# A ninth Strassen pair in gate and up, and three down products whose left operands are made in the down stage

## The chip, the cores and the metric

The kernel runs on one core of a Trainium2 chip. The metric is the device time of one execution in microseconds. A core has a matrix engine (TensorE, PE in the rows, with PEld for its weight loads), a vector engine (VectorE, DVE), an activation engine (ScalarE, ACT), GpSimd (POOL) and a queue engine (SyncE, SP); the DMAs that SP, ACT and POOL issue share sixteen DMA engines. Each engine works through its own instructions in order and waits on semaphores for the others.

## The reference

A trunk of two layers on x of 512 tokens by 1024 channels, in float32. Layer 0 mixes tokens by causal pooling, layer 1 by differential attention; after each mixer comes a SwiGLU feed-forward of width 2816, each with a scaled residual and a LayerNorm.

```python
for i in range(DEPTH):
    h = _multiscale_pool(...) if i % 2 == 0 else _diff_attention(...)
    x = _layernorm(ALPHA * x + h, ln_mix_g[i], ln_mix_b[i])
    x = _layernorm(ALPHA * x + _swiglu(x, w_gate[i], w_up[i], w_down[i]), ln_ffn_g[i], ln_ffn_b[i])

def _swiglu(x, w_gate, w_up, w_down):
    return (jax.nn.silu(x @ w_gate) * (x @ w_up)) @ w_down
```

The change lies in the two feed-forward layers alone.

## The kernel before

**Three matmuls for one.** Every float32 operand is held as two parts, a high one (a cast by ScalarE) and a low one (the rest, made by VectorE as the value less the high part). A product is high by high, high by low and low by high (`mm3`, line 180). So each 128x1024 chunk of weights that arrives costs one ScalarE cast and one VectorE subtraction (`split`, line 148) before PE can use it. There is another way (line 164, for thirteen chunks of the attention stage): ScalarE casts the chunk and writes its negative into the low part, and a DMA from GpSimd adds the chunk from memory once more, so VectorE has no work with it.

**Gate and up.** The 2816 hidden channels are 22 blocks of 128. Block k and block k + 11 form pair k, eleven pairs in all. A pair is worked in one of two ways. A *plain* pair is two pieces f (f0 and f1 are pair 0, f2 and f3 pair 1, f4 and f5 pair 2), each with one gate and one up product of 24 matmuls over 512 tokens (`plain`, line 986; `gated` multiplies them). A *Strassen* pair p takes seven products in place of eight half-size ones, each of 24 matmuls over 256 tokens (`strassen`, line 1006; `half_product`, line 908). Its weights are sums of the four chunks that arrive (VectorE, line 697), and its right operands sums of quarters of x (`sums_of_x`). Three pairs are plain, eight are Strassen's. The first two of the eight (`PRE`) have two of their seven products at the start of the stage and five later. `ORDER` sets the order of the pieces; `steps` holds the sums, casts and low parts ahead of PE by the lookahead of `ahead`.

**What the down stage needs from before.** The down product is Strassen's too: seven products P1, Q5, P6, Q3, P7, P2, Q4 (`DOWN`), each of six *items* (`PAIRS`: five with two blocks, one with one), 42 items in all, numbered d_0 to d_41 (P6 is d_12 to d_17, Q3 d_18 to d_23, P7 d_24 to d_29). An item has a *weight* (sums of down weights, or a block of them) and a *left* operand (sums of quarters of the hidden values), each in two parts. The weight sums are made during gate and up (`weight_sums`, `sum_terms`, line 814): GpSimd loads the terms of set k, adds one by DMA, VectorE adds twice (lines 816 and 817), ScalarE's queue stores to `tsum`. The lefts of Q3 and P7 are made there too: after each pair, `sum_hidden` (line 836) makes two sums on VectorE (lines 842 to 845), ScalarE casts them, VectorE makes the low halves (line 849) and ScalarE's queue stores both parts to `ssum`.

**The down stage.** `multiply` (line 1075) runs an item's matmuls: 12 of 512 columns for two blocks. Ahead of it `prepare(j + 5, j + 4)` (line 890) makes the weight of item j + 4 (`split_item`, line 858: cast on ScalarE, low part on VectorE) and the left of item j + 3 (`left`, line 871). There are six weight pairs, so a weight's tiles come free when PE has ended the item six before. Lefts of Q3 and P7 are loaded from `ssum` by GpSimd (line 878). The left of P6 is subtracted in place by VectorE (line 886), then cast and split; the other lefts are cast and split as they are. Between products VectorE adds results into the residual (line 1073) and takes statistics (line 222). The affine step of the preceding LayerNorm on the residual (lines 260 and 261) is done in half gate and up, half the down stage (`AFFINE`).

## Time and profile before

| what | value |
|---|---|
| three timed runs, us | 934.22, 936.23, 933.59 |
| their median, us | 934.22 |
| the profiled execution: span from first to last instruction, us | 933.1 |
| mean granted TensorE clock | 0.998 |
| HBM read, written | 179.96 MB, 36.72 MB |
| layer 0 gate and up | about 34 to 265 us |
| layer 0 down | 265 to about 364 us |
| attention | about 364 to 593 us |
| layer 1 gate and up, down, end | about 593 to 821, to about 910, to 933 us |

For the profiled execution the profile gives the span alone. A row of the timeline gives start, duration, engine, source line, operation, what is written and read, and in brackets how long the engine stood idle before it and what ended that. A row of the windows gives busy time of each engine in a stretch with the count of instructions, the granted clock, the DMA engines' busy share and GB/s. A row of the chain gives start, duration, engine, what is written, line and count. Matmul durations in a timeline row overlap, so the pace of PE is taken from chain rows.

### The profile page before, as it was taken

The page shows a single profiled execution, that of the slowest core. Times are in us where ns is not written, and L with a number is a line of the kernel's source. Part 1 is how long each engine was busy: PE and PEld are TensorE (multiplying, and loading weights), DVE is VectorE, ACT ScalarE, POOL GpSimd, SP SyncE. Part 2 cuts the span into 40 slices and gives each one's busy share as a digit, 9 for nine tenths or more (in the row PEclk, how much of TensorE's full clock was granted, in tenths as well). Part 3 has the DMA queues.
Part 4 walks back from the last instruction along what each step waited for, and adds up shares of the span by engine and source line. Part 5 has one row for each costly group of instructions (what it writes and reads, how often), then busy time and mean ns, then how long its engine had stood idle before and what let it go on. Part 6 is the DMA issues. An engine that isn't in the chain of part 4 may idle for free.

```text
span 933.1 us, 14897 instructions
## 1 busy us (share of the span) xinstructions
PE 921.9 (99%) x5662; PEld 824.1 (88%) x5662; DVE 798.9 (86%) x1185; ACT 521.0 (56%) x827; POOL 127.8 (14%) x153
## 2 busy tenths in 40 slices
PE   8999999999999999999999999999999999999996
PEld 8998989999988888888888888988999999988885
DVE  6989798999878887968989886889798999977888
ACT  6663444455554456776878863843445554654361
POOL 4131211110101201200211100201112110001101
PEclk9999999999999999999999999999999999999999
DMA  8388999986869989876576522487899996869963
GB/s 236 116 278 263 297 290 299 293 265 230 259 197 312 357 279 250 221 190 171 143 157 157 152 88 84 136 290 217 265 300 303 268 302 204 257 205 329 360 209 101
DMA packets 87909, 217.65 MB, mean 233 GB/s; under 512 B 15348, under 2 KB 26868, under 8 KB 87838
## 3 DMA queue, kind: packets, MB, share of 16 engines
q1 hardware_dynamic: 45148, 123.46, 39.2%
q0 software_dynamic: 18912, 58.47, 25.5%
q10 hardware_dynamic: 23778, 34.78, 10.5%
q8 instruction: 44, 0.72, 0.3%
q14 instruction: 27, 0.22, 0.1%
HBM read 179.96 MB, written 36.72 MB: 232 GB/s over the span
## 4 chain that ended last, share of the span: by engine, by line
PE 86%; DVE 8%; ACT 3%; issue 1%; DMA 1%; ACTq 0%; POOL 0%; DVEq 0%; POOLq 0%
PE A L919 18%; PE P L1086 14%; PE C L919 9%; PE Q L1086 6%; PE B L919 5%; PE va L1242 2%; PE s L1311 2%; PE q L181 2%; PE q L183 2%; PE k L181 2%; PE k L183 2%; PE q L182 2%; PE k L182 2%; PE u L181 1%; PE u L183 1%
## 5 line engine op out<-in xcount | busy, mean ns | idle before, releaser
L697 DVE TENSOR_TENSOR raw<-raw,raw 128x1024 f32<-128x1024 f32 x64 | 78.0, 1221 | 6.8 <-DMA raw<-in_wall 5.9
L155 ACT CAST xs<-hid 128x512 fp32r<-128x512 f32 (+1 forms) x60 | 34.7, 581 | 24.4 <-DVE hid L886 24.4
L156 DVE TENSOR_TENSOR xs<-hid,xs 128x512 fp32r<-128x512 f32 (+1 forms) x60 | 38.3, 641 | 7.8 <-ACT xs L155 7.8
L1331 ACT ACTIVATE p<-p,mn 128x128 f32<-128x128 f32 (+3 forms) x64 | 35.3, 552 | 14.1 <-DVE mn L1326 14.1
L847 ACT CAST v<-u 128x512 fp32r<-128x512 f32 x22 | 13.7, 621 | 43.4 <-DVE u L845 43.4
L878 POOL DMA_DIRECT2D xs<-ssum x24 | 17.5, 727 | 140.3 <-PE Q L1086 67.9
L810 POOL DMA_DIRECT2D b<-in_wall x20 | 15.1, 813 | 142.2 <-DVE g_23l L703 33.2
L810 POOL DMA_DIRECT2D hid<-in_wall x24 | 19.0, 834 | 98.7 <-DMA tsum<-hid 27.4
L1326 DVE CUSTOM_DVE_ANT_0 p<-s,bias 128x128 f32<-128x128 f32 (+3 forms) x64 | 28.0, 485 | 1.1 <-PE s L1311 1.1
L231 POOL TENSOR_TENSOR rs<-rs,mhalf 128x1 f32<-128x1 f32 x16 | 12.6, 787 | 103.6 <-DVE rs L230 96.2
L282 ACT ACTIVATE y<-pt,bT,gT 128x128 f32<-128x128 f32 x40 | 15.1, 456 | 15.9 <-PE pt L268 15.8
L222 DVE BATCH_NORM_STATS2 st<-res 128x6 f32<-128x512 f32 x32 | 22.2, 694 | 1.1
L1028 ACT COPY hid<-C 128x512 f32<-128x512 f32 x16 | 9.4, 588 | 23.6 <-PE C L919 14.1
L762 ACT CAST xs<-hid 128x1024 fp32r<-128x1024 f32 x8 | 8.4, 1051 | 22.0 <-DVE hid L780 10.6
L811 POOL DMA_DIRECT2D b<-in_wall x10 | 12.3, 1228 | 60.8 <-DMA b<-in_wall 60.8
L1042 ACT ACTIVATE sg<-A 128x512 f32<-128x512 f32 x16 | 9.5, 596 | 19.5 <-PE A L919 19.5
L811 POOL DMA_DIRECT2D hid<-in_wall x12 | 14.8, 1236 | 35.5 <-DMA hid<-in_wall 35.5
L1345 DVE SCALAR_TENSOR_TENSOR p<-p,sm,p 128x128 f32<-128x128 f32 (+3 forms) x32 | 17.6, 551 | 1.1
L156 POOL TENSOR_TENSOR sql<-sq,sqh 128x512 fp32r<-128x512 f32 x7 | 9.3, 1329 | 60.5 <-ACT sqh L155 60.5
L1035 DVE TENSOR_TENSOR hid<-C,hid 128x512 f32<-128x512 f32 x16 | 11.0, 688 | 7.4 <-PE C L919 4.9
L261 DVE TENSOR_TENSOR res<-res,gb 128x512 f32<-128x512 f32 (+1 forms) x20 | 16.0, 799 | 0.7
L849 DVE TENSOR_TENSOR v<-u,v 128x512 fp32r<-128x512 f32 x22 | 15.1, 685 | 1.4 <-ACT v L847 1.4
(1212 smaller groups left out, 3583.6 us busy)
## 6 DMA issues: line engine op xcount, KB each, us to landing
raw<-in_wall SPq DMA_DIRECT2D x130, 512.0 KB, 5.5
r<-tsum SPq DMA_DIRECT2D x40, 512.0 KB, 4.3
hid<-in_wall POOLq DMA_DIRECT2D x36, 512.0 KB, 6.0
b<-in_wall POOLq DMA_DIRECT2D x30, 512.0 KB, 6.8
r<-in_wall SPq DMA_DIRECT2D x30, 512.0 KB, 6.1
tsum<-hid ACTq DMA_DIRECT2D x24, 512.0 KB, 6.2
ssum<-v ACTq DMA_DIRECT2D x22, 512.0 KB, 4.7
tsum<-b ACTq DMA_DIRECT2D x20, 512.0 KB, 4.7
```

What stands on the lines that cost most here:

```text
L155: nc.scalar.copy(dst_h, src)
L156: (low or nc.vector).tensor_tensor(dst_l, src, dst_h.bitcast(F32), op=ALU.subtract)
L181: nc.tensor.matmul(acc, ah, bh, start=start, stop=False)
L182: nc.tensor.matmul(acc, ah, bl, start=False, stop=False)
L183: nc.tensor.matmul(acc, al, bh, start=False, stop=stop)
L697: tt(t, raws[pair[0]], raws[pair[1]], op=ALU.add)
L810: nc.gpsimd.dma_start(out=t[:, j], in_=src[:, j])
L811: nc.gpsimd.dma_start(out=t[:, 0], in_=src[:, :, 1], accum_op=ALU.add)
L919: nc.tensor.matmul(acc[:, f * 256 : (f + 1) * 256], w[:, c], x[:, kk, :], start=start and i == 0, stop=stop and i == len(todo) - 1, skip_g ...
L1086: nc.tensor.matmul(accs[s], x[:, k, r], y[:, c], start=first and k == 0 and e == 0, stop=last and k == m - 1 and e == 2, skip_group_check= ...
L1326: nc.vector.tensor_tensor_reduce(out=p, in0=accs[c], in1=biases[h][:, w - 1 :: -1] if w < S else biases[h][:, ::-1], op0=ALU.add, op1=ALU. ...
L1331: nc.scalar.activation(p, p, AF.Exp, bias=mn[:, q, c : c + 1], scale=-1.0, accum_out=sm[:, q, c : c + 1],)
```

## The change

Pair 1 (f2 and f3) stays plain, pair 2 becomes a Strassen pair, and the order of the first pieces is new. `sum_hidden` keeps one subtraction in place, which P6 and the others need, and no longer makes, casts or stores anything; `ssum` is gone. In the down stage `left` makes Q3's left as the sum of a quarter of the hidden values and P6's left, and P7's as the negative of P6's left less another quarter; both are then cast and split like the rest. For items 0, 2 and 4 of P6, Q3 and P7 (`BY_DMA`) the weight's low part is made by ScalarE and an accumulating DMA. All eight halves of the affine step come after f3 and p4 to p10. Weight sums begin one piece later and follow every piece from f1 to p9; the odd sets use a tile of their own instead of rows of `hid` or the tile of the LayerNorm's scales.

```diff
-SPLIT = (3, 4, 5, 6, 7, 8, 9, 10)
+SPLIT = (2, 3, 4, 5, 6, 7, 8, 9, 10)
-SUMS = 1
-NO_SUMS = (3, 3, 10)
-SPARED = {2: 6}
+SUMS = {1: (2, 1), 2: (2, 1)}
+NO_SUMS = ("f0", "p10")
+BY_DMA = {"P6": (0, 2, 4), "Q3": (0, 2, 4), "P7": (0, 2, 4)}
-ORDER = "f0 f1 f2 f3 p3 f4 p4 f5 p5 p6 p7 p8 p9 p10".split()
+ORDER = "f0 f1 f2 p2 f3 p3 p4 p5 p6 p7 p8 p9 p10".split()
-AFFINE = {("P6", 2): (0, 1), ("P6", 3): (1, 1), ("Q3", 1): (2, 0), ("Q3", 2): (3, 0)}
+AFFINE = {u: (i // 2, i % 2) for i, u in enumerate("f3 p4 p5 p6 p7 p8 p9 p10".split())}
...
             def sum_hidden(k):
-                first, second = hid[:, k, :256], hid[:, k, 256:]
-                a12, a22 = hid[:, k + HALF, :256], hid[:, k + HALF, 256:]
...
-                tt(u[:, 0, :], first, second, op=ALU.subtract)
-                tt(second, second, a22, op=ALU.subtract)
-                tt(u[:, 1, :], a12, first, op=ALU.subtract)
-                tt(u[:, 1, :], u[:, 1, :], second, op=ALU.add)
-                yield
-                nc.scalar.copy(v[:, :, 0, :], u)
-                yield
-                tt(v[:, :, 1, :], u, v[:, :, 0, :].bitcast(F32), op=ALU.subtract)
-                yield
-                nc.scalar.dma_start(out=ssum[:, :, :, k, :], in_=v.bitcast(F32))
+                tt(hid[:, k, 256:], hid[:, k, 256:], hid[:, k + HALF, 256:], op=ALU.subtract)
...
             def split_item(j):
...
-                if final and j == len(items) - 1:
+                if i in BY_DMA.get(p, ()) or final and j == len(items) - 1:
                     nc.scalar.copy(h, drops[j])
                     nc.scalar.mul(l, drops.pop(j), -1.0)
-                    nc.gpsimd.dma_start(
-                        out=l, in_=tsum[2, len(PAIRS) - 1, :, :w].bitcast(F32R), accum_op=ALU.add
-                    )
+                    nc.gpsimd.dma_start(out=l, in_=source(j).bitcast(F32R), accum_op=ALU.add)
                 else:
                     split(h, l, drops.pop(j))
...
-                if p in ("P7", "Q3"):
-                    nc.gpsimd.dma_start(out=t.bitcast(F32), in_=ssum[:, 0 if p == "P7" else 1, :, r, :])
...
+                if p == "P6":
+                    tt(src, hid[:, r, 256:], src, op=ALU.subtract)
+                elif p == "Q3":
+                    src = fp.tile([P, 2, 256], F32, tag="u", name=f"u{layer}_{j}")[:, :m]
+                    tt(src, hid[:, q, :256], hid[:, r, :256], op=ALU.add)
+                elif p == "P7":
+                    nc.vector.scalar_tensor_tensor(
+                        src, src, -1.0, hid[:, q, 256:], op0=ALU.mult, op1=ALU.subtract
+                    )
+                split(t[:, 0], t[:, 1], src)
...
             for kind, i in units(layer):
                 (plain if kind == "f" else strassen)(i)
+                unit = f"{kind}{i}"
+                if unit not in NO_SUMS:
+                    weight_sums()
+                if unit in AFFINE:
+                    affine(n - 1, *AFFINE[unit])
```

How the instructions stand is shown at three places. In the rows, d_12h and d_12l are the high and low part of item 12's weight, r_12 is the chunk that arrived for it, xs holds the lefts and hid the hidden values.

On ScalarE in layer 0's down stage, from item 12 (the first of P6), before:

```order
L155 CAST d_12h<-r_12_3086 128x1024
L155 CAST xs_538<-hid_537 128x256
L155 CAST d_13h<-r_13_3106 128x1024
L155 CAST xs_538<-hid_537 128x512
L155 CAST d_14h<-r_14_3124 128x1024
L155 CAST xs_538<-hid_537 128x512
L155 CAST d_15h<-r_15_3144 128x1024
```

and in the changed kernel:

```order
L846 CAST d_12h<-r_12_3097 128x1024
L847 ACTIVATE d_12l<-r_12_3097 128x1024
L155 CAST xs_538<-hid_537 128x256
L155 CAST d_13h<-r_13_3117 128x1024
L155 CAST xs_538<-hid_537 128x512
L846 CAST d_14h<-r_14_3135 128x1024
L847 ACTIVATE d_14l<-r_14_3135 128x1024
L155 CAST xs_538<-hid_537 128x512
```

Every second weight has a second ScalarE pass over its chunk, which stands ahead of the next left's cast.

On VectorE at the passage from P6 to Q3 in the same stage (L886 and L1073 are P6's left and the residual addition), before:

```order
L156 TENSOR_TENSOR d_17l<-r_17_3187,d_17h 128x512
L886 TENSOR_TENSOR hid_537<-hid_537 128x2x256
L156 TENSOR_TENSOR xs_538<-hid_537,xs_538 128x512
L156 TENSOR_TENSOR d_18l<-r_18_3208,d_18h 128x1024
L886 TENSOR_TENSOR hid_537<-hid_537 128x256
L156 TENSOR_TENSOR xs_538<-hid_537,xs_538 128x256
L260 TENSOR_TENSOR res<-res,gb_3164 128x512
L261 TENSOR_TENSOR res<-res,gb_3164 128x512
L156 TENSOR_TENSOR d_19l<-r_19_3229,d_19h 128x1024
```

and in the changed kernel (L865 is P6's left, L868 Q3's):

```order
L156 TENSOR_TENSOR d_17l<-r_17_3196,d_17h 128x512
L865 TENSOR_TENSOR hid_537<-hid_537 128x2x256
L156 TENSOR_TENSOR xs_538<-hid_537,xs_538 128x512
L865 TENSOR_TENSOR hid_537<-hid_537 128x256
L156 TENSOR_TENSOR xs_538<-hid_537,xs_538 128x256
L156 TENSOR_TENSOR d_19l<-r_19_3239,d_19h 128x1024
L868 TENSOR_TENSOR u_18_3327<-hid_537 128x512
L156 TENSOR_TENSOR xs_538<-u_18_3327,xs_538 128x512
L868 TENSOR_TENSOR u_19_3350<-hid_537 128x512
L156 TENSOR_TENSOR xs_538<-u_19_3350,xs_538 128x512
L156 TENSOR_TENSOR d_21l<-r_21_3278,d_21h 128x1024
```

The low parts of items 18 and 20 and the affine rows are gone from VectorE, and each left of Q3 has its sum and its low part there.

On VectorE at the end of pair 5 in layer 0's gate and up (the gate's products L1055 and L1056, the down weights' sums L816 and L817, weights' low parts g), before:

```order
L1055 TENSOR_TENSOR hid_537<-sg_5_0_1771,hid_537 128x2x256
L1056 TENSOR_TENSOR hid_537<-sg_5_1_1797,hid_537 128x2x256
L816 TENSOR_TENSOR hid_537<-hid_537 128x512
L817 TENSOR_TENSOR hid_537<-hid_537 128x512
L703 TENSOR_TENSOR g_38l<-raw_1642,g_38h 128x1024
L842 TENSOR_TENSOR u_5_1846<-hid_537 128x256
L843 TENSOR_TENSOR hid_537<-hid_537 128x256
L844 TENSOR_TENSOR u_5_1846<-hid_537 128x256
L845 TENSOR_TENSOR u_5_1846<-u_5_1846,hid_537 128x256
L703 TENSOR_TENSOR g_39l<-raw_1478,g_39h 128x1024
L703 TENSOR_TENSOR g_40l<-raw_1674,g_40h 128x1024
L849 TENSOR_TENSOR v_5_1847<-u_5_1846,v_5_1847 128x2x256
```

and in the changed kernel (the same sources stand at L1028, L1029, L814 and L815):

```order
L1028 TENSOR_TENSOR hid_537<-sg_5_0_1827,hid_537 128x2x256
L1029 TENSOR_TENSOR hid_537<-sg_5_1_1853,hid_537 128x2x256
L835 TENSOR_TENSOR hid_537<-hid_537 128x256
L814 TENSOR_TENSOR hid_537<-hid_537 128x512
L815 TENSOR_TENSOR hid_537<-hid_537 128x512
L260 TENSOR_TENSOR res<-res,gb_530 128x512
L261 TENSOR_TENSOR res<-res,gb_530 128x512
L703 TENSOR_TENSOR g_41l<-raw_1699,g_41h 128x1024
```

Four operations of the hidden sums and one low half have left the pair's end; one subtraction and a half of the affine step have come.

81 lines of the change are left out of this document (26 added, 55 removed).

## The prediction

> **What bounds the kernel now.** I read the page's head first, then the chain of waits, then the busy time by stage.
>
> ```profile
> span 933.1 us, 14897 instructions
> PE 921.9 (99%) x5662; PEld 824.1 (88%) x5662; DVE 798.9 (86%) x1185; ACT 521.0 (56%) x827; POOL 127.8 (14%) x153
> 605.53 5.47 PE g L725 x24
> 649.08 2.87 PE A L919 x24
> 309.98 14.96 PE Q L1086 x66
> 324.94 38.08 PE P L1086 x168
> 92.00:144.00 52.00, 51.13 (x338) 46.97 (x337) 44.73 (x55) 21.65 (x27) 7.91 (x9) 1.00 0.91 282
> 182.00:222.00 40.00, 40.00 (x334) 39.88 (x334) 38.79 (x49) 20.68 (x27) 2.96 (x4) 1.00 0.82 252
> 295.00:310.00 15.00, 15.00 (x68) 12.43 (x67) 12.18 (x18) 8.09 (x11) 4.35 (x6) 1.00 0.92 326
> 310.00:325.00 15.00, 15.00 (x67) 12.39 (x67) 12.89 (x16) 5.21 (x6) 3.62 (x5) 1.00 0.96 364
> ```
>
> TensorE is the bound. It idles 11.2 us of 933.1, and the chain shows its pace: 24 matmuls of 512 columns take 5.47 us where they start (38.08 / 168 = 0.227 us each in the long run), 24 of 256 columns take 2.88 us (0.120 each). So there are two ways to move the time: fewer or cheaper matmuls, or operands that come late. The window rows (columns: window, PE, PEld, DVE, ACT and POOL busy with counts, clock, DMA share, GB/s) say how near the second is. VectorE is busy 38.8 of 40 us in the middle of gate and up; PE loses 0.9 us in the window from 92 to 144, and nothing in the down stage, where DMA is 92 to 96% busy.
>
> **What the change takes off PE.** By the orders, each layer loses 96 matmuls of 512 columns (one pair's plain products) and gains 168 of 256 columns (seven half products). 96 x 0.227 = 21.8 us, 7 x 2.88 = 20.2 us: 1.6 us a layer, **3.2 us** in all. Nothing lies beside it, since PE is the bound.
>
> **Gate and up: what VectorE gives and gets.**
>
> ```profile
> 59.13 0.40 PE L181 MATMUL g<-xt,g_6h 128*128 128x512 f32 x1
> 60.36 0.69 DVE L260 TENSOR_TENSOR res<-res,gb 128x512 f32<-128x512 f32 x1
> 67.56 1.23 DVE L703 TENSOR_TENSOR g_9l<-raw,g_9h 128x1024 fp32r<-128x1024 f32 x1 [0.93 <-ACT g_9h L700]
> 116.75 1.23 DVE L703 TENSOR_TENSOR g_19l<-raw,g_19h 128x1024 fp32r<-128x1024 f32 x1 [1.17 <-ACT g_19h L700]
> 120.23 0.42 DVE L842 TENSOR_TENSOR u<-hid 128x256 f32<-128x256 f32 x1
> 121.82 1.22 DVE L703 TENSOR_TENSOR g_22l<-raw,g_22h 128x1024 fp32r<-128x1024 f32 x1
> 123.70 0.69 DVE L816 TENSOR_TENSOR b<-b 128x512 f32<-128x512 f32 x1
> 109.34 1.23 DVE L697 TENSOR_TENSOR raw<-raw,raw 128x1024 f32<-128x1024 f32 x1 [2.37 <-DMA raw<-in_wall]
> 111.96 1.23 DVE L697 TENSOR_TENSOR raw<-raw,raw 128x1024 f32<-128x1024 f32 x1 [1.40 <-DMA raw<-in_wall]
> ```
>
> Four operations of a pair's hidden sums take 1.6 us (120.23 to 121.82) and the low half of v about 0.6, eleven times a layer; one of 0.4 stays. That frees 11 x 1.8 = 20 us of VectorE. The new pair adds four weight sums, three low halves and two half-row operations, 7 x 1.14 + 2 x 0.6 = 9 us (a 1.22 us operation lets the next start after 1.14, as 0.69 lets it after 0.60), and the moved affine steps 4 x 1.3 = 5 us. VectorE ends some 6 us a layer lighter, hidden under PE either way.
>
> The new order asks for the weight sums sooner: p2 comes after f2. From layer 0's first gate (60.4 us) to the low half that p4's third product needs, the new VectorE order holds 37 operations of 1.14, nine of 0.60, three of 0.35 and ten of 0.66: 55 us. PE needs that half 66 us on (f1 starts at 59.1; two plain pieces and p2 end at 95.3, f3 106.2, p3 120.6, two products more 126.4). In the like stretch of before, 60.4 to g_19l's end, VectorE stood in seven waits, from g_9l's 0.93 to g_19l's 1.17, about 8 us together; the two for DMA above are 3.8 of them. 55 + 8 leaves 3 us. Bounds: 0.9 us is gained if no loss stays, 3 us are lost if the 8 become 14 (rival 3). I take 0.
>
> **The down stage: where I expect the loss.** Operands of item j are made while PE is five items back, because six weight pairs rotate. One item of two blocks is 12 matmuls, 2.72 us. For P6 the trace shows the ring that makes them:
>
> ```profile
> 282.81 1.05 ACT L155 CAST d_12h<-r 128x1024 fp32r<-128x1024 f32 x1 [0.60 <-PE Q L1086]
> 285.53 1.05 ACT L155 CAST d_13h<-r 128x1024 fp32r<-128x1024 f32 x1 [1.36 <-PE Q L1086]
> 289.17 0.62 ACT L155 CAST xs<-hid 128x512 fp32r<-128x512 f32 x1 [2.59 <-DVE hid L886]
> 289.69 1.04 ACT L155 CAST d_14h<-r 128x1024 fp32r<-128x1024 f32 x1
> 290.77 1.23 DVE L156 TENSOR_TENSOR d_14l<-r,d_14h 128x1024 fp32r<-128x1024 f32 x1 [0.26 <-ACT d_14h L155]
> 291.91 0.68 DVE L886 TENSOR_TENSOR hid<-hid 128x512 f32<-128x512 f32 x1
> 300.41 0.62 ACT L155 CAST xs<-hid 128x512 fp32r<-128x512 f32 x1 [2.74 <-DVE hid L886]
> 300.94 0.62 ACT L155 CAST d_17h<-r 128x512 fp32r<-128x512 f32 x1
> 303.52 1.04 ACT L155 CAST d_18h<-r 128x1024 fp32r<-128x1024 f32 x1
> 294.85 0.39 PE L1086 MATMUL P<-d_12h,xs 128*128 128x512 f32 x1
> 309.81 0.39 PE L1086 MATMUL Q<-d_18h,xs 128*128 128x512 f32 x1
> 335.88 0.39 PE L1086 MATMUL P<-d_28l,xs 128*128 128x512 f32 x1
> ```
>
> Cast of a left operand to cast of the next weight 0.52, to its low half 1.08, to the next left sum 1.14, to that one's cast about 0.72: 3.46 us an item against PE's 2.72. So P6 already eats its lead: weight 13 is cast 12.0 us ahead of its use (285.53 against 297.57, one item after 294.85), weight 18 only 6.3. Q3 and P7 now win it back, as their lefts come by DMA. The change makes Q3 and P7 like P6 and takes three low halves of each product off VectorE; ScalarE writes the negated weight instead, and an accumulating DMA finishes it. What that costs, the attention stage shows (its own by-DMA weights):
>
> ```profile
> 413.40 1.05 ACT L165 CAST w81h<-raw 128x1024 fp32r<-128x1024 f32 x1
> 414.35 1.06 ACT L166 ACTIVATE w81l<-raw 128x1024 fp32r<-128x1024 f32 x1
> 415.70 0.87 POOL L167 DMA_DIRECT2D w81l<-in_wall  x1 [19.51 <-ACT w81l L166]
> DMA to landing us min/median/max: 6.1/7.5/9.7
> DMA to landing us min/median/max: 5.8/7.4/12.8
> DMA to landing us min/median/max: 4.6/6.4/7.7
> ```
>
> The three landing rows are, in turn, these thirteen accumulates of 512 KB (line 167), the 22 accumulates of gate and up (line 811), and the plain loads of lefts that GpSimd issued in layer 0's down stage (line 878).
>
> Ring for two items, one by DMA and one not: cast to weight cast 0.52, to the negation 0.95, to the next left's cast 0.95, to the other weight's cast 0.52, to its low half 1.08, to the left sum 1.14, to its cast 0.72 = 5.9 us, against PE's 5.44. A pair with the half item takes 5.0 (0.62 for 1.05 and 0.60 for 1.14) and the one after it 5.7, with 0.7 more where the two residual additions stand between. That is 5.9 + 5.0 + 5.7 + 0.7 = 17.3 us a product; PE takes 14.96. From the cast of d_12 at 282.8 (the same as before, where ScalarE waits for PE) I get 300.7 for d_18 (the first product 17.8, with the start's waits), 318.0 for d_24 and 329.6 for d_28. The negation ends 2.0 us after: 331.6. PE wants its low half at 335.88. **4.3 us are there; needed are 0.3 to the issue (415.41 to 415.70) and the landing.** The nearest row in kind and load is line 811's, 7.4: short by 3.4 us. Shortfalls of items before it are part of the same 3.4, because PE's delay gives lead back. The ends: 4.6 (a plain load) leaves 0.6, 5.8 gives 1.8, 9.7 gives 5.7. Two layers, the same code, the like DMA share: **6.8 us** (1.2 to 11.4).
>
> [...]
>
> What else moves costs nothing, with its cover: twelve loads of lefts a layer go and nine accumulates come, so GpSimd's queue holds fewer issues; eleven stores of v go from ScalarE's queue; the affine rows that leave the down stage give VectorE 5 us there, outside the ring; the final scale's load moves ahead, where its tile is free. Without PE's cover of gate and up, the 9 us of the new pair's vector work would be the price.
>
> **Sum.** 933.1 - 3.2 + 0 + 6.8 = 936.7 for the profiled span. The runs' median, 934.22, is 1.1 above that span, so 937.8.
>
> **The rivals.**
> [...]
> 2. *Even.* Landing of 5.5 to 6.9 us: 1.5 to 3 us lost a layer, 931.0 + 3.0 to 931.0 + 6.0 = 934 to 937. For it: the plain loads' 6.4 in this very stage. Against it: both accumulate rows have medians of 7.4 and more.
> 3. *The early order starves.* In layer 0 VectorE stands at p3's weight sums until the accumulate of that set has landed. Store 6.2, load 6.0 and accumulate 7.4 follow one another there, some 21 us with issues, between two sets that the new order puts 15 us of PE time apart (p2 to p3). It decides from 6 us of such waiting; PE loses what exceeds the 3 us left, 3 us. On top of the forecast: 941. Before, sets 3 and 5 stood 23 us apart on VectorE (123.70 and 146.91), with no wait.
>
> ```profile
> 146.91 0.68 DVE L816 TENSOR_TENSOR b<-b 128x512 f32<-128x512 f32 x1
> tsum<-hid ACTq DMA_DIRECT2D x24, 512.0 KB, 6.2
> hid<-in_wall POOLq DMA_DIRECT2D x36, 512.0 KB, 6.0
> ```
>
> **Numbers.** About 0.3%, 2.8 us, can be told from no change. The forecast (landing above 7 us) has 0.45, rival 3 0.07, rival 2 0.25, rival 1 0.23. Hence slower 0.52, within 0.25, faster 0.23. The likeliest case alone spans 937 to 942.5; with both signs the range goes from rival 1's 931 to the 9.7 us landing, 931 + 11.4 = 942.4.
>
> **What would show it.** PE matmuls of P7 (and the end of Q3) that wait for a low half written by DMA, first at d_18 to d_24, up to 3.4 us a layer; the first five products of the down stage taking 78 us a layer instead of 74.8; GpSimd's issues of d_28l at about 332; gate and up 1.6 us shorter a layer, the window from 92 to 144 still with under 1 us of idle PE. [...]

## The result and the profile after

The changed kernel takes 946.33 us (median of 4 runs, 944.15 to 948.28) against 933.9 us of the kernel before beside it (932.43 to 936.23): a ratio of 1.014, 95% interval 1.0121 to 1.0159. It is slower, and 4 us above the upper end of the predicted range. The profiled execution took 948.28 us, the longest of the four, and the stages below, which are read from it, sum to 13.4 us, 1 us more than the medians differ by. Here is the head of the page after:

```profile
span 946.5 us, 15095 instructions
...
PE 923.6 (98%) x5806; PEld 830.3 (88%) x5806; DVE 788.2 (83%) x1145; ACT 546.4 (58%) x859; POOL 125.5 (13%) x147
```

From its chain of waits, the rows where PE's pace changes (start, duration, the bank of PE's result memory that is written, matmuls):

```profile
131.51 5.49 PE C L905 x24
137.00 3.14 PE A L905 x24
140.14 2.88 PE B L905 x24
```

And the windows that were shown of before, with the same columns:

```profile
92.00:144.00 52.00, 48.22 (x336) 45.95 (x335) 42.66 (x47) 21.74 (x26) 10.80 (x12) 0.93 0.94 298
182.00:222.00 40.00, 40.00 (x336) 40.00 (x335) 36.19 (x40) 19.04 (x25) 2.72 (x3) 1.00 0.71 212
295.00:310.00 15.00, 15.00 (x67) 12.41 (x67) 10.16 (x16) 9.88 (x13) 1.68 (x2) 1.00 0.99 249
310.00:325.00 15.00, 13.17 (x57) 10.24 (x55) 10.27 (x15) 9.13 (x14) 2.51 (x3) 1.00 1.02 261
325.00:340.00 15.00, 13.29 (x56) 10.47 (x57) 10.71 (x16) 9.09 (x12) 1.68 (x2) 1.00 0.94 243
```

PE's idle time has doubled, from 11.2 to 22.9 us (946.5 - 923.6). In layer 0 it lies in two places: 3.8 us in the window from 92 to 144, where the mean clock is 0.93 as well (24 half matmuls that elsewhere take 2.88 us took 5.49 and 3.14), and 1.8 and 1.7 us in the windows of Q3 and P7. PE's waits over both layers, in total, times and longest (us), name them:

```profile
PE C L905 <- ACT hid L1003: 5.1, 2, 2.8
PE Q L1061 <- DMA d_20l<-in_wall: 2.9, 2, 1.6
PE P L1061 <- DMA d_26l<-tsum: 2.6, 2, 1.7
...
PE A L905 <- DVE hid L1012: 0.9, 1, 0.9
PE Q L1061 <- DMA d_22l<-in_wall: 0.6, 1, 0.6
PE P L1061 <- DMA d_24l<-tsum: 0.4, 1, 0.4
```

The next table counts from one fixed matmul of PE to another: layer 0's gate and up from the transposes behind its first half product (9 us into the stage), layer 1's from f0's first full-width product, the down stage from its first matmul; the five down products are P1 to P7.

| stage, us | before | changed | difference | predicted |
|---|---|---|---|---|
| gate and up, layer 0 | 221.9 | 225.6 | +3.7 | -1.6 |
| five down products, layer 0 | 74.8 | 79.4 | +4.6 | +3.4 |
| gate and up, layer 1 | 215.3 | 217.4 | +2.1 | -1.6 |
| five down products, layer 1 | 74.8 | 78.6 | +3.8 | +3.4 |
| all else | 346.3 | 345.5 | -0.8 | 0 |

The down stage went as forecast and somewhat further. Gate and up, taken at no loss, lost 5.3 and 3.7 us against its forecast. What stands there at p4, the third Strassen pair, in layer 0 (VectorE, then ScalarE, then PE in the timeline; start, duration, and idle time before with its releaser):

```profile
124.42 1.23 DVE L703 TENSOR_TENSOR g_24l<-raw,g_24h 128x1024 fp32r<-128x1024 f32 x1
125.56 0.68 DVE L1028 TENSOR_TENSOR hid<-hid 128x512 f32<-128x512 f32 x1
...
127.23 0.68 DVE L814 TENSOR_TENSOR hid<-hid 128x512 f32<-128x512 f32 x1
...
128.56 1.22 DVE L697 TENSOR_TENSOR raw<-raw,raw 128x1024 f32<-128x1024 f32 x1
129.86 1.04 ACT L700 CAST g_28h<-raw 128x1024 fp32r<-128x1024 f32 x1 [4.01 <-DVE raw L697]
130.87 0.58 ACT L1003 COPY hid<-C 128x512 f32<-128x512 f32 x1
131.51 0.79 PE L905 MATMUL C<-xs,g_25h 128*128 128x256 f32 x2 [2.84 <-ACT hid L1003]
```

p4's fourth product goes into the bank of its second, which ScalarE must copy out first (L1003). On ScalarE's queue that copy stands behind the cast of g_28h, p4's seventh operand, which waits 4.01 us for VectorE's sum. VectorE makes that sum behind p3's last results (from 125.56) and a row of weight sums (the two adds of one set, L814 and L815), without a gap.

### The profile page after: what moved, and what is told of

Same layout as the page of the kernel before. It is cut to its first block, busy times and chain, and to the rows that moved or that the text cites. A ratio compares the mean times of both kernels' runs of the same rounds, so it can differ in the third digit from the quotient of the medians.

```text
span 946.5 us, 15095 instructions
## 1 busy us (share of the span) xinstructions
PE 923.6 (98%) x5806; PEld 830.3 (88%) x5806; DVE 788.2 (83%) x1145; ACT 546.4 (58%) x859; POOL 125.5 (13%) x147
## 4 chain that ended last, share of the span: by engine, by line
PE 76%; DVE 11%; DMA 5%; issue 4%; ACT 4%; ACTq 0%; DVEq 0%; POOL 0%; POOLq 0%
PE A L905 19%; PE C L905 10%; PE P L1061 9%; PE B L905 5%; PE Q L1061 2%; DMA d_26l<-tsum 2%; PE s L1282 2%; DVE raw L697 1%; PE q L181 1%; PE q L183 1%; PE k L181 1%; PE k L183 1%; PE q L182 1%; PE k L182 1%; PE u L181 1%
## 5 line engine op out<-in xcount | busy, mean ns | idle before, releaser
L697 DVE TENSOR_TENSOR raw<-raw,raw 128x1024 f32<-128x1024 f32 x72 | 87.8, 1221 | 5.9 <-DMA raw<-in_wall 4.8
L156 DVE TENSOR_TENSOR xs<-hid,xs 128x512 fp32r<-128x512 f32 x72 | 46.1, 642 | 21.6 <-ACT xs L155 21.6
L155 ACT CAST xs<-hid 128x512 fp32r<-128x512 f32 x72 | 41.6, 580 | 30.0 <-DVE hid L870 17.9
L808 POOL DMA_DIRECT2D b<-in_wall x24 | 18.0, 793 | 154.6 <-DMA tsum<-b 78.1
L808 POOL DMA_DIRECT2D hid<-in_wall x20 | 15.0, 751 | 104.7 <-DVE hid L814 40.8
L1003 ACT COPY hid<-C 128x512 f32<-128x512 f32 x18 | 10.6, 587 | 29.4 <-PE C L905 21.1
L1005 ACT COPY hid<-A 128x512 f32<-128x512 f32 x18 | 10.6, 587 | 27.0 <-PE A L905 27.0
L1017 ACT ACTIVATE sg<-A 128x512 f32<-128x512 f32 x18 | 10.7, 596 | 23.7 <-PE A L905 23.7
L809 POOL DMA_DIRECT2D b<-in_wall x12 | 14.7, 1227 | 62.5 <-DMA b<-in_wall 62.5
L1012 DVE TENSOR_TENSOR hid<-hid,A 128x512 f32<-128x512 f32 x18 | 12.3, 681 | 7.0 <-PE A L905 6.9
L156 POOL TENSOR_TENSOR sql<-sq,sqh 128x512 fp32r<-128x512 f32 x7 | 9.3, 1326 | 60.2 <-ACT sqh L155 60.2
L261 DVE TENSOR_TENSOR res<-res,gb 128x512 f32<-128x512 f32 (+1 forms) x20 | 16.0, 799 | 0.7
L260 DVE TENSOR_TENSOR res<-res,gb 128x512 f32<-128x512 f32 (+1 forms) x20 | 15.8, 791 | 0.0
L156 DVE TENSOR_TENSOR xs<-u,xs 128x512 fp32r<-128x512 f32 (+1 forms) x12 | 7.8, 648 | 9.6 <-ACT xs L155 9.6
```

Source lines behind the costliest of these rows:

```text
L155: nc.scalar.copy(dst_h, src)
L156: (low or nc.vector).tensor_tensor(dst_l, src, dst_h.bitcast(F32), op=ALU.subtract)
L697: tt(t, raws[pair[0]], raws[pair[1]], op=ALU.add)
L808: nc.gpsimd.dma_start(out=t[:, j], in_=src[:, j])
```

## Experiments on the down stage

The table gives every run: the median, the ratio to the kernel before beside it with its 95% interval, and the stages as above. In a kernel with added lines the profile's line numbers stand up to 15 higher than in the changed kernel.

| run | us | ratio, interval | gate and up 0 | down 0 | gate and up 1 | down 1 |
|---|---|---|---|---|---|---|
| changed kernel | 946.3 | 1.0140 (1.0121-1.0159) | 225.6 | 79.4 | 217.4 | 78.6 |
| e10_leftfirst | 958.1 | 1.0269 (1.0247-1.0291) | 223.3 | 88.8 | 217.4 | 83.1 |
| e4_nodma | 960.3 | 1.0294 (1.0274-1.0315) | 223.3 | 86.0 | 217.5 | 86.2 |
| e13_sumearly | 938.0 | 1.0056 (1.0042-1.0071) | 224.7 | 74.8 | 217.4 | 76.3 |
| e14_two | 938.1 | 1.0058 (1.0041-1.0075) | 224.5 | 74.8 | 216.4 | 75.6 |
| e5_eight | 941.4 | 1.0090 (1.0072-1.0108) | 220.4 | 78.8 | 216.3 | 78.6 |
| e1_queue | 946.0 | 1.0137 (1.0114-1.0160) | 224.8 | 79.2 | 216.9 | 78.5 |
| e21_steps | 946.1 | 1.0133 (1.0113-1.0153) | 223.6 | 79.0 | 217.7 | 79.4 |
| e7_affine | 944.4 | 1.0122 (1.0106-1.0139) | 223.6 | 81.1 | 216.1 | 78.8 |
| e18_relief | 950.5 | 1.0193 (1.0172-1.0214) | 223.5 | 79.1 | 220.3 | 79.5 |
| e23_three | 935.1 | 1.0026 (1.0012-1.0039) | 224.0 | 74.8 | 217.9 | 75.3 |
| e24_three_two | 935.5 | 1.0023 (1.0012-1.0035) | 222.3 | 74.8 | 216.3 | 74.8 |
| e31_noadds | 930.8 | 0.9959 (0.9945-0.9974) | 220.3 | 74.8 | 215.1 | 74.8 |
| e32_noaccum | 935.5 | 1.0016 (1.0002-1.0030) | 223.2 | 74.8 | 217.9 | 74.8 |
| e33_f2late | 935.7 | 1.0017 (1.0002-1.0031) | 223.1 | 74.8 | 216.8 | 74.8 |
| e36_order_all | 937.4 | 1.0045 (1.0030-1.0061) | 224.9 | 74.8 | 217.0 | 74.9 |
| e35_order | 948.8 | 1.0165 (1.0148-1.0182) | 224.7 | 79.1 | 220.0 | 78.4 |
| e38_pooladds | 955.9 | 1.0235 (1.0210-1.0259) | 233.8 | 74.8 | 224.5 | 75.9 |
| e39_pooladds2 | 949.6 | 1.0173 (1.0143-1.0203) | 226.8 | 74.8 | 222.3 | 75.5 |

The changed kernel, e10, e4, e13 and e14 have the same code in gate and up. Their layer 0 values, 223.3 to 225.6, show how far single executions differ there, so a difference of up to 2 us between two rows of that column proves nothing; medians decide. Much of the spread is PE's clock: behind the wait at p4 two products took 5.49 and 3.14 us in the changed kernel at a clock of 0.50, and 3.14 and 2.88 in e10, where it stayed at 1.00 (see the last section).

**The left operand ahead of the weights.** In `prepare`:

```diff
+                while prepared[1] < min(lefts, prepared[0]):
+                    left(prepared[1])
+                    prepared[1] += 1
                 while prepared[0] < min(upto, len(items)):
```

> Only the order inside the function that prepares the down stage's items is changed: the left operand of item j+3 is made ahead of the weights of item j+4, not behind them. In the changed kernel ScalarE's cast of a left operand waits 1.89 us at every second item for VectorE's sum (L865, L868, L870), which stands behind the low half (1.22 us) of the item before, which waits for ScalarE's cast of it: a ring of 5.7 to 5.9 us for two items, against 5.44 us that PE takes for them; so the accumulate of d_20l is issued at 310.39 and lands some 7.7 us later, when PE has been waiting. THEORY (the ring through both engines is the loss of the down stage): with the sum ahead, the ring is cut; ScalarE's work for two items is 3 x 0.95 + 2 x 0.52 = 3.9 us, so the casts start when their buffers come free, about 13 us ahead of PE, of which casts, issue and landing take 2 + 0.4 + 9.3 = 11.7 at most. The five first products take 74.8 to 75.3 us a layer instead of 79.44 and 78.64, no PE wait for a d low half is left in P6 to P7, and the time is 946.3 - 8.0 = 938.3 us (937 to 940). RIVAL 1 (an accumulate that lands in 7 to 9 us is too late from any start the buffers allow): the PE waits stay, and at most 2 us comes back, 944 to 946. RIVAL 2 (the left operands' own buffers then stop the queue, PE waits for a left operand in place of a weight): 942 to 948.

It took 958.1 us, 12 more than the changed kernel, so all three expectations missed. ScalarE's casts of left operands and of the weights between them, in its timeline:

```profile
295.66 0.62 ACT L155 CAST xs<-hid 128x512 fp32r<-128x512 f32 x1 [3.87 <-DVE hid L865]
...
303.12 1.04 ACT L155 CAST d_19h<-r 128x1024 fp32r<-128x1024 f32 x1
306.06 0.62 ACT L155 CAST xs<-u 128x512 fp32r<-128x512 f32 x1 [1.90 <-DVE u L868]
...
309.00 1.04 ACT L155 CAST d_21h<-r 128x1024 fp32r<-128x1024 f32 x1
```

From d_19 to d_21 it is again 5.88 us: the edit turns the circle (cast, low half, sum, cast of the left) by half a step and does not cut it. Besides, the left's cast now stands first in ScalarE's queue where VectorE waits for a product's end, and stood 3.87 us. PE then waited up to 3.82 us.

**No low half by transfer.** VectorE makes all of them.

```diff
-BY_DMA = {"P6": (0, 2, 4), "Q3": (0, 2, 4), "P7": (0, 2, 4)}
+BY_DMA = {}
```

> The nine low halves a layer that an accumulating transfer makes are made by VectorE as all others; all else is the changed kernel. THEORY (the ring is set by the left operands that are made in the stage, not by the transfers): without the transfers each two-block item of P6, Q3 and P7 has the chain low half 1.14, sum 0.61, cast of the left operand 0.52, cast of the weight 0.95, together 3.2 to 3.5 us against PE's 2.72, over 18 items some 13 us a layer, of which the five items of lead take about 8: the five first products take 79 to 83 us a layer, the time is 945 to 953 us, and PE waits for low halves by VectorE. RIVAL (the transfers' landing of 7.7 us is the loss, the ring keeps up without them): the five first products take 75 to 76 us a layer, and the time is 946.3 - 7.5 = 938.8 us (937 to 941).

960.3 us, with the five products at 86.0 and 86.2. Without the transfers the stage is 7 us a layer worse, so they spare more than they cost. PE now waits for ScalarE's casts of lefts alone (13 waits, 11.4 us in both layers), not for VectorE's low halves as the theory said. Its direction held; its 79 to 83 us were too few.

**The sums one item earlier.** This cuts the circle; Q3's sum goes into the second half of its row, free by then:

```diff
+            def sum_left(j):   # P6's, Q3's or P7's sum of item j, as in left()
+                ...
             def left(j):
-                if p == "P6": ...
+                if j + 1 < len(items):
+                    sum_left(j + 1)
                 split(t[:, 0], t[:, 1], src)
```

> The run before, with the left operand ahead of the weights, did not cut the ring: sum, cast of the left operand, cast of the weight, low half follow one another in a circle, and turning the circle by half a step left it 5.88 us for two items. Here VectorE's sum of a left operand is made one item earlier (Q3's sum into the freed second half of its row), so that ScalarE's cast of it waits for no low half. The nine transfers a layer stay. THEORY OF THE TRANSFERS: in the changed kernel the DMA engines are the bound of P6 to P7: from 300 to 336 us their busy share is 0.99; 3.15 MB of accumulates took 50.2% of them and 6.00 MB of plain loads 48.9%, that is 3.0 us of all 16 engines for an accumulate of 512 KB and 1.5 for a load of it; a product needs 5.5 x 1.5 + 3 x 3.0 = 17.3 us of them against 14.96 of PE; Q3 and P7 took 17.41 and 17.13. Then earlier casts only make the accumulates wait longer: landing rises above 8.5 us, Q3 and P7 still take 16.5 to 17.4 us, the time is 944 to 947 us. THEORY OF THE RING (the prediction's): with the ring cut, P6, Q3 and P7 take 14.96 to 15.2 us each, no PE wait for a low half, and the time is 946.3 - 8.0 = 938.3 us.

The theory of the ring forecast 938.3 us; it took 938.03. PE waits nowhere in layer 0's down stage. ScalarE's timeline:

```profile
303.42 1.05 ACT L846 CAST d_20h<-r 128x1024 fp32r<-128x1024 f32 x1 [1.15 <-issue]
304.38 1.05 ACT L847 ACTIVATE d_20l<-r 128x1024 fp32r<-128x1024 f32 x1
305.34 0.60 ACT L155 CAST xs<-hid 128x512 fp32r<-128x512 f32 x1
306.14 1.05 ACT L155 CAST d_21h<-r 128x1024 fp32r<-128x1024 f32 x1 [0.20 <-ACT xs L155]
307.10 0.61 ACT L155 CAST xs<-hid 128x512 fp32r<-128x512 f32 x1
308.86 1.05 ACT L846 CAST d_22h<-r 128x1024 fp32r<-128x1024 f32 x1 [1.15 <-issue]
```

The windows of P6 to P7:

```profile
295.00:310.00 15.00, 15.00 (x68) 12.40 (x67) 11.21 (x18) 11.56 (x16) 2.52 (x3) 1.00 1.04 297
310.00:325.00 15.00, 15.00 (x68) 12.43 (x67) 11.21 (x18) 11.55 (x16) 2.52 (x3) 1.00 1.05 302
325.00:340.00 15.00, 15.00 (x68) 12.43 (x67) 12.46 (x18) 9.73 (x14) 0.83 (x1) 1.00 0.95 293
```

No cast waits for VectorE; items pass in 5.44 us a pair (303.42 to 308.86), PE's own pace, and d_20 is cast 3 us sooner against PE than in the changed kernel (4.67 us earlier, of which PE itself is 1.62). The accumulates did not land faster: from issue to landing they took 7.9 to 9.2 us by item (means of the two layers), against 7.2 to 8.6 for d_20 to d_28 of the changed kernel. There was time for them. In layer 1 1.4 us of the loss are left: PE waits 0.86 us there at d_12, whose accumulate took 10.7 us. This also ends the theory of the transfers. A busy share of 0.99 to 1.02 had looked like DMA engines at their limit at 249 to 261 GB/s; the same transfers now ran at 297 to 302 GB/s.

**Two transfers a product.** The same with `(0, 3)` for `(0, 2, 4)` in `BY_DMA`.

> As the run with the sums one item earlier, but two low halves a product by transfer (items 0 and 3 of P6, Q3 and P7), not three; VectorE makes the other four. THEORY OF THE TRANSFERS: a product needs 5.5 x 1.5 + 2 x 3.0 = 14.3 us of the DMA engines, under PE's 14.96; VectorE has 4 x 1.14 + 6 x 0.61 + 6 x 0.61 + 1.3 = 13.2 us a product; so Q3 and P7 take 15.0 to 15.3 us each, the five first products 75 to 75.6 us a layer, and the time is 946.3 - 7.5 = 938.8 us (937.5 to 940.5), while three transfers with the same order of sums stay above 943. THEORY OF THE RING: both kernels with the earlier sums come out alike, at 938 to 940. RIVAL (VectorE's own order is the bound: its low halves wait for casts, 13.2 us cannot be packed into 14.96): 942 to 946, PE waiting for low halves or left operands from VectorE and ScalarE.

938.06 us, as with three. With the ring cut, neither the transfers nor VectorE's extra low halves bind, but for 0.47 us at d_12 in layer 1; the claim that three would stay above 943 fell with its theory.

**The down stage's part alone.** Eight pairs, in the old order:

```diff
-SPLIT = (2, 3, 4, 5, 6, 7, 8, 9, 10)
-NO_SUMS = ("f0", "p10")
-ORDER = "f0 f1 f2 p2 f3 p3 p4 p5 p6 p7 p8 p9 p10".split()
+SPLIT = (3, 4, 5, 6, 7, 8, 9, 10)
+NO_SUMS = ("f0", "f3", "p10")
+ORDER = "f0 f1 f2 f3 p3 f4 p4 f5 p5 p6 p7 p8 p9 p10".split()
```

> The change of the down stage alone: left operands made there, nine low halves by transfer, the rows of the norm's scale in gate and up; but eight Strassen pairs, in the order of the kernel before. THEORY (the two losses are apart: the down stage costs its 4.6 and 3.8 us whatever gate and up does, and p4's stall came with the ninth pair and its order): the five first products take 78.6 to 79.5 us a layer, gate and up takes 221 to 222 us a layer as before, and the time is 934 + 8.4 = 942.4 us (941 to 944). RIVAL 1 (the rows of the norm's scale that the change moves into gate and up, 1.4 us a unit of VectorE, make the stall, with or without the ninth pair): gate and up has a wait of 2 to 3 us and a low clock behind it here too, 946 to 951. RIVAL 2 (the freed vector work, 11 units of 3.8 us, shortens gate and up): under 941.

941.4 us, at 942.4 forecast: the two losses are apart. Down costs 4.0 and 3.8 us here too; gate and up has no wait in layer 0 and one of 0.96 us in layer 1. So the ninth pair and its order bring p4's stall, not the moved affine rows.

## Experiments on gate and up

**The copy ahead of the cast.**

```diff
-    return 4 if k in PRE else 6
+    return 4 if k in PRE or (k, p) == (4, "P1") else 6
```

> One order on ScalarE's queue is changed in gate and up: at p4's first product two casts fewer are put ahead, so that the copy of p4's second product out of its bank stands ahead of the cast of the seventh operand (g_28h) and not behind it. In the changed kernel that cast waited 4.01 us for VectorE's sum, the copy stood behind it, and PE waited 2.84 us (layer 0) and 2.21 us (layer 1) for the copy; right after, the granted clock read 0.50 for some us. THEORY (one queue order makes the whole loss of gate and up): both waits and both falls of the clock go; gate and up, from its first matmul to the first d_0, comes out at 220.0 to 220.6 us a layer instead of 225.6 and 224.0, and the time at 946.3 - 9.1 = 937.2 us (936 to 939). RIVAL 1 (VectorE is late in this stretch whatever stands where: it runs without a gap from 116 to 134 us): the wait moves to p4's fifth or sixth product, behind g_26l or g_27l, and less than 3 us comes back: 943 to 946. RIVAL 2 (the wait goes, but the low clock has another cause than the wait): only the 5.0 us of the two waits comes back, 941, and the clock still reads 0.5 at about 131 us.

946.04 us. PE's wait at p4's fourth product falls to 1.04 and 0.42 us, but the last product now waits 2.35 and 2.03 us for VectorE (L1012). Rival 1 holds in kind, as the wait moves and nothing comes back; it moves to the seventh product, not the fifth or sixth.

**Another order of p4's steps**, with which nothing is put off by more than a step:

```diff
+                if k == 4:
+                    order_of = order_of.replace(
+                        "sum 6, cast 5, cast 6, low 4, low 5", "cast 5, low 4, low 5, sum 6, cast 6")
```

> The changed kernel with one order altered: of p4's steps, the sum and the cast of the seventh operand come behind the cast of the sixth and the low halves of the fifth and sixth, so that on ScalarE's queue the copy of p4's second product stands ahead of the cast of g_28h, and on VectorE's the low halves of g_26 and g_27 ahead of the seventh sum. Unlike the first run of this kind, nothing is put off by more than a step. THEORY (PE's wait is for a copy that stands behind a cast that waits for VectorE's late sum): the copy now waits only for the store ahead of it, whose row of weight sums ends at 128.6 us, so PE's wait at p4's fourth product is 0.4 to 1.1 us in place of 2.84 and 2.21, the clock stays at 1.00, and no wait follows at p4's last product, whose low half now ends at about 133 to 135 us, ahead of PE's 137: gate and up gains 1.8 + 2.6 in layer 0 and 1.5 + 1.6 in layer 1: 946.3 - 7.5 = 938.8 us (937.5 to 941). RIVAL (VectorE's arrears of some 4 us at p3's end must be paid by PE wherever the order puts them, as when the wait moved to the last product and took 2.35 and 2.03 us): the waits of gate and up still sum to over 2 us a layer, 942.5 to 946.

946.07 us, and the rival's picture: 1.04 and 0.42 us at the fourth product, 1.82 and 1.81 at the fifth, where the copy of the third product's bank now stands behind that cast.

**Less for VectorE near p4.** First the affine rows that stand behind f3 and p4 moved behind p5 and p7, then one row of weight sums from p2 to p10 besides:

```diff
+AFFINE = {"p5": [(0, 0), (0, 1)], "p6": [(1, 0)], "p7": [(1, 1), (2, 0)], ...}   # e7, e18
-NO_SUMS = ("f0", "p10")
+NO_SUMS = ("f0", "p2")                                                            # e18
```

> The rows of the norm's scale that stand after f3 and p4 (two of VectorE's operations each, 1.37 us) move behind p5 and p7; all else is the changed kernel. In it VectorE runs without a gap from 116 to 134 us, and its seventh sum for p4 ends at 129.8 us when PE's fourth product could have begun at 128.7. THEORY (VectorE is behind there by what the new order puts on it, and the row after f3 at 111.25 us is 1.37 us of it): the wait of PE at p4's fourth product shrinks from 2.84 to about 1.5 us in layer 0 and from 2.21 to about 0.9 in layer 1, the granted clock stays at 1.00 there as after other waits under 1.7 us, and gate and up gains 1.4 + 2.6 us in layer 0 and 1.3 + 1.6 in layer 1: 946.3 - 6.9 = 939.4 us (938 to 942). RIVAL (VectorE is behind because its operands land late: it waited 3.83 us for raw rows at 95 to 98 us while the DMA engines are busy at 0.91 to 0.99, and the 1.37 us only become a longer wait there): the wait of PE stays above 2 us, the clock falls, 945 to 947.

> As the run with the two rows of the norm's scale moved, and besides no row of weight sums after p2, one after p10 in its place: until p4's fourth product VectorE has 1.37 + 1.33 us less to do, and the DMA engines the loads, accumulate and stores of one row of weight sums less. THEORY: p4's wait goes altogether in both layers, and with it the low clock; gate and up takes 220 to 221 us in layer 0 (the changed kernel 225.6, the kernel before 221.9) and two to three us less than the changed kernel's in layer 1; the last weight sums come after p10, and the down stage's second product finds them in time, as it loads them 16 us after its start at the earliest. Time 946.3 - 8.5 = 937.8 us (936.5 to 940). RIVAL (the last row of weight sums now comes late: the down stage's Q5 or P6 waits for its tsum rows): gate and up as said, but 2 to 5 us more in the first two or three products of the down stage, 940 to 943.

e7 took 944.4 us and e18 950.5, and PE's wait at p4 stayed: 2.88 and 2.29 us, then 2.14 and 2.15. In e7 VectorE's sum came 0.9 us earlier, but so did PE, whose wait of 0.94 us at p3's last product had gone. The time moves from one wait to another. Neither time lies in a forecast range of its run, and e18's theory, that the wait goes altogether, is refuted. e18 also made a new wait of its own, 2.00 and 2.56 us at p9: the buffer for one row's terms lies in the rows of `hid` that p9 writes, and p9's copy waited for the store of it:

```profile
231.11 0.59 ACT L1004 COPY hid<-C 128x512 f32<-128x512 f32 x1 [5.62 <-DMA tsum<-hid]
```

**The mends together**: earlier sums, p4's steps, affine rows later; then with two transfers a product.

> Three edits together: the left operands' sums one item earlier, the order of p4's steps, and the two rows of the norm's scale behind p5 and p7. THEORY (the losses are a ring in the down stage, a queue order at p4, and VectorE's arrears there, and all three are now mended): down stage 74.8 us in layer 0 and 75 to 76.3 in layer 1, gate and up 219.8 to 220.8 us in layer 0 (before 221.9) and 1 to 1.6 us under the kernel before's in layer 1; the time is 932.9 - 1.6 - 1.3 + 1.2 = 931.2 us (929.5 to 933), that is 0.995 to 1.000 of the kernel before. RIVAL (the waits in gate and up return elsewhere): 934 to 938.

> As the run with three edits, with two low halves a product by transfer in place of three. THEORY (with the ring cut, neither the transfers nor VectorE is near its limit): the same time within 0.8 us, the first transfer of P6 in layer 1 waits 0.5 us instead of 0.9: 930 to 932. RIVAL (VectorE's 13.2 us a product are too dense beside the other work of layer 1): over 933.

935.13 and 935.45 us, both above their theories: the down stage is whole but for 0.5 us in e23's layer 1, gate and up is not. The times are those of the rivals; e24's rival named layer 1's down stage, which lost nothing. PE's waits at p4 are 1.04 and 1.81, then 0.41 and 1.81 us, as in e21. These are the best kernels found that compute everything, and still 0.2 to 0.3% above the kernel before.

**Where VectorE's delay comes from.** From e24_three_two, one leaves VectorE's adds of four rows out, the other the accumulating transfers of five:

```diff
-                tt(t[:, 1, 1], t[:, 0, 0], t[:, 1, 1], op=ALU.add)
-                tt(t[:, 1, 0], t[:, 1, 1], t[:, 1, 0], op=ALU.add)
+                if k not in (1, 2, 3, 4):   # e31: the two adds
+                    ...
+                if k not in (1, 2, 3, 4, 5):   # e32: the accumulate in load_terms
```

> The run with three edits and two transfers, less the two adds on VectorE of the second to fifth row of weight sums of each layer (after f2, p2, f3 and p3; 1.33 us each): what they would store is wrong, all transfers and waits stay. THEORY A (the arrears at p4 are VectorE's own work): with 5.3 us less by then, and 4.0 us less before p3's end, PE's waits at p4 (1.05 and 1.82 in layer 0, 0.41 and 1.82 in layer 1) go altogether, gate and up gains 2.9 and 2.2 us, and the time is 935.4 - 5.1 = 930.3 us. THEORY B (the arrears come from raw rows that land late): VectorE only waits longer for them, the waits of PE at p4 keep over 1.5 us a layer, and the time is 933 to 935.

> The run with three edits and two transfers, less the accumulating transfer of the second to sixth row of weight sums of each layer (512 KB each, some 3.0 us of all 16 DMA engines): the sums are wrong, VectorE's work is all there. THEORY B (late raw rows): 9 us of the DMA engines less between 63 and 115 us; VectorE's idle 3.8 us for raw rows at 95 to 98 us go or shrink below 1.5, PE's waits at p4 fall by as much, from 2.87 to under 0.6 in layer 0, time 931 to 932.5. THEORY A (VectorE's own work): the waits of PE stay within 0.5 us of 2.87 and 2.23, 934.5 to 935.5.

PE's waits in e31:

```profile
PE A L920 <- ACT hid L1020: 2.3, 2, 1.2
```

PE's waits in e32:

```profile
PE A L920 <- ACT hid L1020: 3.6, 2, 1.8
...
PE C L920 <- ACT hid L1018: 0.8, 2, 0.4
```

And VectorE's wait for raw rows in e32, from 60 to 135 us (4.0 us in e24_three_two):

```profile
DVE raw L702 <- DMA raw<-in_wall: 1.0, 1, 1.0
```

e31 takes 930.8 us, as theory A said (930.3), though one wait of 1.15 us a layer stays. In e32 VectorE's wait for raw rows does shrink, to 1.0 us. PE's waits at p4 shrink by 0.6 us in layer 0, from 2.87 to 2.23, and not at all in layer 1, and the time is that of e24. So it is in the main VectorE's own work near p4 that holds PE up; the wait for a transfer at 95 us, which looked like the cause, is worth at most those 0.6 us.

**Easing the first units, or moving f3.** A row of weight sums less after f2; then f3 between p3 and p4, with the other mends but without p4's steps (e36), and alone (e35):

```diff
-NO_SUMS = ("f0", "p10")
+NO_SUMS = ("f0", "f2")                                                # e33
-                if k % 2 == 0 and k < HALF - 1:
+                if k % 2 == 0 and k < HALF - 3:                       # e33
-ORDER = "f0 f1 f2 p2 f3 p3 p4 p5 p6 p7 p8 p9 p10".split()
+ORDER = "f0 f1 f2 p2 p3 f3 p4 p5 p6 p7 p8 p9 p10".split()             # e36, e35
```

> The run with three edits and two transfers, with no row of weight sums after f2 and one after p10 instead, and the ninth row's terms in the other buffer, so that its store is not in the way of p9's rows of hid. It takes 1.33 us of VectorE and some 3.3 MB of transfers out of f2 to f3. THEORY (either source of the arrears is eased early enough): PE's waits at p4 fall from 2.87 and 2.23 us to under 1 us a layer, no wait follows at p9 or in the down stage's second and third products, and the time is 935.4 - 3.5 = 931.9 us (930 to 933.5), 0.997 to 1.001 of the kernel before. RIVAL (the arrears are structural: p2 and p3 with 14.4 us of PE each hold as much of VectorE, and easing f2 only lets it wait there): 934 to 936.

> The left operands' sums one item earlier, two transfers a product, the two rows of the norm's scale later (as in the run with three edits and two transfers), but p4's steps as in the changed kernel, and f3 between p3 and p4 instead of between p2 and p3. THEORY (PE waits at p4 because VectorE must, within p3's 14.4 us, catch up from a lead of four items to one of six; f3, where VectorE has some 6 us to spare, takes that up): no wait over 1 us at p4, gate and up 219.5 to 220.5 us in layer 0 and 213.5 to 214.5 in layer 1, time 935.4 - 5 = 930.4 us (929 to 932), 0.996 to 0.999 of the kernel before. RIVAL (p2 and p3 back to back run VectorE into the same arrears, now at p3): the waits move to p3's last products, 2 to 4 us a layer, time 933 to 939.

> The changed kernel with f3 between p3 and p4 instead of between p2 and p3, and nothing else. THEORY: gate and up loses its waits and its low clock, 946.3 - 9 = 937.3 us (936 to 939), all of the rest being the down stage. RIVAL (the arrears come at p3): 942 to 948.

935.66, 937.39 and 948.79 us: the rivals' times, the last 0.8 us past its range. Work taken out of f2 takes 0.6 us off p4's first wait in layer 0 and leaves 0.42 and 1.81. With f3 moved, p4 has no wait in e36, and p3 has it instead, at its first product behind p2 and not at its last ones, as the rival had it, alike in both layers (PE's timeline of e36, layer 0):

```profile
95.45 0.50 PE L915 MATMUL A<-xs,g_15h 128*128 128x256 f32 x2 [2.15 <-ACT g_15h L701]
...
96.71 0.58 PE L915 MATMUL A<-xs,g_15l 128*128 128x256 f32 x1 [0.76 <-DVE g_15l L704]
```

So a plain unit does absorb VectorE's delay, as supposed. With f0 and f1 first, as in every order tried, nine pairs leave only f2 and f3 to stand among them, and one gap stays uncovered.

**The adds on GpSimd**, with their stores on its queue, from e24_three_two and from e14_two:

```diff
-                tt(t[:, 1, 1], t[:, 0, 0], t[:, 1, 1], op=ALU.add)
+                nc.gpsimd.tensor_tensor(t[:, 1, 1], t[:, 0, 0], t[:, 1, 1], op=ALU.add)
-                    nc.scalar.dma_start(out=dst[:, j], in_=t[:, j])
+                    nc.gpsimd.dma_start(out=dst[:, j], in_=t[:, j])
```

> The run with three edits and two transfers, with the two adds of every row of weight sums on GpSimd instead of VectorE, and the two stores of it issued from GpSimd's queue instead of ScalarE's. VectorE has 1.33 us a unit less, ScalarE 0.9 us of issues a unit less. GpSimd's adds of 512 columns took 1.33 us where it did others, so 2.7 us a row; its queue waits for loads and stores anyway. THEORY (VectorE's own work at p2 to p4 holds PE up): as with the adds left out, no wait over 1.2 us at p4, gate and up about 220 and 214.5 to 215 us, the time 930 to 931.5 us, 0.996 to 0.999 of the kernel before. RIVAL 1 (GpSimd's row of load, accumulate, adds and store takes longer than the short units f2 and f3 of 10.9 us, and its rows come late to the down stage): a wait in Q5 or P6, 932 to 937. RIVAL 2 (adds of GpSimd slow VectorE's down): VectorE's low halves take more than 1.22 us while they run, 932 to 935.

> The same move of the adds and stores to GpSimd, on the run with earlier sums and two transfers alone (p4's steps and the rows of the norm's scale as in the changed kernel; that run took 938.06 us). THEORY: the copy of p4's second product still stands behind the cast of g_28h, but VectorE's seventh sum is 1.33 us or more earlier there and the store is out of ScalarE's queue: PE's wait falls from 2.85 and 2.21 us to 0.5 to 1.5, the clock stays at 1.00, time 931 to 933. RIVAL (VectorE only waits for PE's products instead, as when the rows of the norm's scale were moved and PE's wait stayed at 2.88): 935 to 938.

955.9 and 949.6 us: rival 2 of e38's expectation, and far dearer than its 932 to 935; e39 missed both of its forecasts. GpSimd's two adds in e38's timeline:

```profile
128.11 1.80 POOL L819 TENSOR_TENSOR hid<-hid 128x512 f32<-128x512 f32 x1
129.99 2.14 POOL L820 TENSOR_TENSOR hid<-hid 128x512 f32<-128x512 f32 x1
```

VectorE's operations beside them:

```profile
126.70 1.22 DVE L708 TENSOR_TENSOR g_26l<-raw,g_26h 128x1024 fp32r<-128x1024 f32 x1
127.84 3.17 DVE L708 TENSOR_TENSOR g_27l<-raw,g_27h 128x1024 fp32r<-128x1024 f32 x1
130.93 2.29 DVE L702 TENSOR_TENSOR raw<-raw,raw 128x1024 f32<-128x1024 f32 x1
```

VectorE's low half takes 3.17 us instead of 1.22, its sum 2.29. The two lose 1.95 and 1.07 us beside a row whose adds cost VectorE 1.33 us itself, so the move costs VectorE more than it saves.

## Why the prediction was wrong, point by point

- **PE's 3.2 us.** Borne out as far as it can be seen: in e31 the sum of both layers' gate and up is 1.85 us under the kernel before (-1.63 and -0.22), with 1.15 us of PE's wait left in each.
- **"Gate and up: I take 0"** is the step that failed; it was 9 us in the profiled execution (5.3 and 3.7). Its working counted VectorE's operations up to the low half for p4's third product, g_24l, and found 3 us to spare. That count itself was near: the stretch held the 37 long operations counted, the operations took 57 us, not 55, and VectorE's waits 10.1, not 8. The half ended at 125.65 us and PE's first matmul with it began at 125.87, when PE had already stood 0.94 us at p3's last product; so some 0.7 us were wanting in place of 3 to spare, which is within the bounds given. The error was to stop there. Behind that half VectorE had p3's results, a row of weight sums and the seventh sum, to 129.8 us, and PE's next product hung on that sum by way of a copy queued on ScalarE behind its cast. A pair's steps are made six items ahead, so more is due at p4 than its third product needs; the count had to run through p4, and through ScalarE's queue.
- **The clock** was in no step. In the changed kernel the waits account for about 2.9 us of layer 0's loss (0.94 + 2.84 less 0.87 of before) and 2.2 of layer 1's; the rest, 2.4 and 1.5 us, is near what the two products behind them took too long (5.49 + 3.14 less 2 x 2.88, or 2.9 us, in layer 0; by layer 1's rows of the same chain, 4.44 + 3.05 less the same, or 1.7). Of these, 0.26 us stand behind such a wait at full clock too (3.14 and 2.88 in e10). So some 4 of the 9 us came with the low clock, which the same code does not always meet: e10 and e4 took 223.3 us in layer 0, 3.0 above the forecast and not 5.3. Without those 4 us this execution would still lie near 944 us, outside the range.
- **The down stage, 6.8 us**, was right in its mechanism and 1.6 us short (4.6 + 3.8). The casts came where the ring put them: d_18, d_24 and d_28 at 302.43, 319.73 and 331.28 us, that is 300.7, 318.0 and 329.6 plus the 1.8 us by which the stage began later. For d_28, for which the sum was made, it held: the accumulate took 7.7 us in both layers against the 7.4 taken, and landed 3.9 and 3.6 us later than PE would have wanted it without a wait, against 3.4. Mis-sized was the landing of the item before it by transfer, d_26: 9.0 us in layer 0 and 8.2 in layer 1, so that it came 4.4 and 3.6 us late and set the loss. The waits at d_20 and d_22 are part of that, as the prediction said of earlier items. That the ring, and not the transfers, is the cause is shown by e13, where the same transfers landed no faster and layer 0's loss was gone.
- **The rivals.** The 931 us of rival 1, from which the range and rival 2 start, are 934.2 - 3.2, a down stage without loss. No run of a kernel that computes everything shows that time; the best took 935.13 us. Rivals 1 and 2 are refuted by PE's waits at the low halves, by landings of 7.7 us in the median and by the losses of 4.6 and 3.8 us. The third, in which VectorE starves for an accumulate of a set of weight sums, is refuted in its mechanism: VectorE never stood at L814, and e32, without five of those accumulates a layer, ran no faster than e24.

Open is whether some other order of VectorE's work fits nine pairs; no order tried here did. The 1.15 us that PE still waits in e31 are again a copy that stands behind: in layer 0 the copy of the third product's bank, at 130.53 us, follows the casts of g_28h and g_29h on ScalarE, the first of which waited 3.76 us for VectorE's seventh sum. That order came with e21's steps; whether e31 would lose the wait without them was not tried.
